# A hybrid decoder layer: the conv's taps, the sums for the FFN, the GroupNorm and one RWKV chain get other places in the order

## The chip, the cores and the metric

One core of a Trainium2 chip runs the whole kernel. The metric is the device time of one execution in microseconds (us); the time of a kernel is the median of its runs. Engines: TensorE (PE) multiplies, VectorE (DVE), ScalarE (ACT) and GpSimd (POOL) work on tiles, SyncE (SP) issues the DMA transfers. Each engine works through its own instructions in order.

## The reference, cut to what matters

One decoder layer on x of shape (1, 1024, 1024), all fp32. One combined projection feeds three groups whose outputs are concatenated and go through one output projection; a gated FFN follows.

```python
def reference(x, w_in, w_out, norm_mix, ...):
    h = rms_norm(x, norm_mix[i])
    proj = h @ w_in[i]
    p_conv, p_nsa, p_rwkv = jnp.split(proj, splits, axis=-1)
    y_conv = conv_mixer(p_conv, ...)      # GLU, depthwise conv of width 31, LayerNorm, swish
    y_nsa = nsa_mixer(p_nsa, ...)         # 8 heads, compressed + selected + sliding-window branches
    y_rwkv = rwkv7_mixer(p_rwkv, ...)     # 4 heads x 64, decay and delta rule, GroupNorm, gate
    mix = jnp.concatenate([y_conv, y_nsa, y_rwkv], axis=-1)
    x = x + mix @ w_out[i]
    h = rms_norm(x, norm_ffn[i])
    x = x + conv_ffn(h, ...)              # silu(causal_dwconv(h @ w_gate)) * (h @ w_up) @ w_down
    return rms_norm(x, norm_final)

def causal_dwconv(x, w, b):               # here k = 31, 256 channels
    y = lax.conv_general_dilated(x, w[:, None, :], window_strides=(1,), padding=[(k - 1, 0)], ...)
    return y + b
```

The RWKV step is, for each time step, S = S * w + (S @ -kk)(kk * a) + v k and y = S r; the kernel does it in chunks.

## The kernel before, in words

Every fp32 matmul of a projection is made of three passes over a high and a low part of each operand (`mm3`, L229). A weight is loaded, ACT writes its high part (`whi`, L120) and DVE the low part (`wlo`, L121); results that are kept go through the same pair on eviction (keys: L689 on ACT, L690 on DVE). A projection of 128 columns takes 24 such matmuls for each half of the 1024 time steps.

`build` walks through a list of steps: the projections (`lora`, `r0`, `keys`, `q`, `r1a`, `cmp0`, ...), and between them the RWKV steps. RWKV works on four units: head pair j (0, 1) times time half h (0, 1). For a unit `S` prepares and builds its matrices, and at its end GpSimd solves a triangular system by forward substitution, 31 rounds of a product (L532) and a sum (L534). `V` (solve) carries the result through DRAM to another layout (DVE copies `sTT`, SP stores and loads, first used at L554) and multiplies it out. `C` (chain) is the recurrence over eight chunks, each a row of PE, DVE, PE, DVE (L595, L596, L601, L608), and at its end the GroupNorm: sums and rsqrt on DVE (L621 to L632), transposes on PE (L635), gating, a store to the DRAM tensor `md` (L642).

The conv has 256 channels in two halves. Half 0 is 31 DVE taps over 1024 columns (L272). Half 1 is, for each tap, two scaled copies on ACT (`ctap`, L278, two buffers) that GpSimd adds up (L279). Then comes the LayerNorm over channels and a store to `md`. Attention goes over eight tiles of 128 queries in the order 7, 6, 5, 4, 0, 3, 2, 1; among them lie the units S10 to C11, and GpSimd makes sums of ffn_down weights (`down_sums`). The out-projection loads `mix` from `md` (L988), which holds the outputs of all three groups.

The order on each engine is set by a scheduler that puts instructions by priority and by a clock of its own; RWKV steps have a high priority, and `issue_after(ins)` keeps instructions out until `ins` has been put. So the order is fixed when the kernel is built, and an engine waits for its next instruction even if a later one could run.

## Time and profile before

| | |
|---|---|
| median of 3 runs | 1477.12 us (1475.97 to 1485.69) |
| profiled execution | 1478.54 us, span 1476.7 us |
| mean granted clock of TensorE | 0.973 |
| PE busy | 1388.3 us, 94% of the span |
| DVE / ACT / POOL busy | 1000.4 / 686.0 / 499.0 us |
| DMA | 186.69 MB, mean 126 GB/s |

The span is the profiled execution from its first instruction to its last. Times in rows are microseconds from the span's start. A busy time is the union of an engine's instructions; the granted clock is the share of full speed (2.4 GHz) that TensorE was given, so 0.50 is its lower level of 1.2 GHz. A number in brackets behind a row is the time that the engine stood idle before it, with the instruction that ended the wait.

### The profile page before, as it was taken

The page shows a single profiled execution, that of the slowest core. Times are in us where ns is not written, and L with a number is a line of the kernel's source. Part 1 is how long each engine was busy: PE and PEld are TensorE (multiplying, and loading weights), DVE is VectorE, ACT ScalarE, POOL GpSimd, SP SyncE. Part 2 cuts the span into 40 slices and gives each one's busy share as a digit, 9 for nine tenths or more (in the row PEclk, how much of TensorE's full clock was granted, in tenths as well). Part 3 has the DMA queues.
Part 4 walks back from the last instruction along what each step waited for, and adds up shares of the span by engine and source line. Part 5 has one row for each costly group of instructions (what it writes and reads, how often), then busy time and mean ns, then how long its engine had stood idle before and what let it go on. Part 6 is the DMA issues. An engine that isn't in the chain of part 4 may idle for free.

```text
span 1476.7 us, 22756 instructions
## 1 busy us (share of the span) xinstructions
PE 1388.3 (94%) x7897; PEld 1096.1 (74%) x7897; DVE 1000.4 (68%) x2187; ACT 686.0 (46%) x1377; POOL 499.0 (34%) x607
## 2 busy tenths in 40 slices
PE   6999588999799999999999899999999999999997
PEld 5887466777576676766777677888788788888886
DVE  5337594454868688798367767677775776666685
ACT  5432246634466655678333433343343334445463
POOL 1001996931153156220001144443444442113310
...
GB/s 182 44 107 83 43 103 91 148 98 168 165 33 118 98 154 119 165 158 87 229 142 64 29 94 93 113 103 69 103 112 93 108 100 166 392 277 210 190 91 114
DMA packets 206679, 186.69 MB, mean 126 GB/s; under 512 B 56355, under 2 KB 145764, under 8 KB 206564
## 3 DMA queue, kind: packets, MB, share of 16 engines
...
q14 instruction: 53, 0.43, 0.1%
...
## 4 chain that ended last, share of the span: by engine, by line
PE 78%; DVE 9%; DMA 4%; POOL 4%; ACT 3%; issue 2%; SPq 1%; DVEq 0%; ACTq 0%
PE gb L229 13%; PE mm L229 13%; PE ga L229 9%; PE rw L229 9%; PE gc L229 8%; PE tr L229 5%; PE tr L922 4%; PE av L930 4%; PE mm L897 2%; DMA mix<-md 2%; PE mm L898 2%; POOL sT L534 1%; POOL sx L532 1%; POOL cacc L279 1%; DVE pp L915 1%
## 5 line engine op out<-in xcount | busy, mean ns | idle before, releaser
L229 PE MATMUL mm<-hT,whi 128*128 128x512 f32 x608 | 200.0, 408 | 18.4 <-DVE ev L690 15.1
L229 PEld LDWEIGHTS mm<-hT,whi 128*128 128x128 f32 x608 | 115.6, 193 | 48.0 <-ACT whi L120 18.8
L229 PE MATMUL mm<-hT,wlo 128*128 128x512 f32 x304 | 123.1, 407 | 2.8 <-DVE wlo L121 2.8
L925 ACT ACTIVATE pT<-tr 128x512 f32<-128x512 f32 (+1 forms) x152 | 79.8, 536 | 58.0 <-PE tr L922 57.7
L930 PE MATMUL av<-pT,V 128*64 128x128 f32 x1056 | 97.3, 289 | 3.9 <-ACT pT L925 3.8
L922 PE MATMUL tr<-idn,pp 128*128 128x128 f32 x528 | 90.7, 290 | 1.8 <-DVE pp L915 1.8
L279 POOL TENSOR_TENSOR cacc<-cacc,ctap 128x512 f32<-128x512 f32 x60 | 85.7, 1440 | 12.6 <-ACT ctap L278 12.6
L121 DVE TENSOR_TENSOR sp<-rb,sp 128x512 fp32r<-128x512 f32 x66 | 57.0, 863 | 46.7 <-ACT sp L120 46.7
L229 PE MATMUL rw<-sp,sp 128*128 128x512 f32 x330 | 86.0, 389 | 0.0
L229 PE MATMUL tr<-sp,sp 128*128 128x512 f32 x330 | 85.9, 389 | 0.0
L930 PEld LDWEIGHTS av<-pT,V 128*64 128x64 f32 x1056 | 60.2, 138 | 30.0 <-issue 12.5
L229 PE MATMUL rw<-woh,mix 128*128 128x512 f32 x240 | 76.7, 394 | 3.7 <-DVE xn L1005 2.7
L922 PEld LDWEIGHTS tr<-idn,pp 128*128 128x128 f32 x528 | 56.2, 142 | 30.8 <-issue 29.4
L897 PE MATMUL mm<-KH,QS 128*128 128x512 f32 (+2 forms) x192 | 75.8, 401 | 3.0 <-DVE mx L901 2.5
L120 ACT ACTIVATE sp<-rb 128x512 fp32r<-128x512 f32 x66 | 41.6, 631 | 73.8 <-PE tr L229 37.5
L121 DVE TENSOR_TENSOR sp<-b,sp 128x512 fp32r<-128x512 f32 x88 | 72.1, 828 | 5.4 <-ACT sp L120 5.0
L915 DVE TENSOR_SCALAR pp<-pp,sm 128x640 f32<-128x640 f32 (+7 forms) x128 | 74.5, 622 | 1.0
L229 PEld LDWEIGHTS mm<-hT,wlo 128*128 128x128 f32 x304 | 58.7, 193 | 19.0 <-DVE wlo L121 4.6
L1084 POOL TENSOR_TENSOR S<-wraw,wr 128x512 f32<-128x512 f32 x22 | 28.5, 1297 | 127.6 <-DVE wlo L121 46.8
L229 PEld LDWEIGHTS rw<-sp,sp 128*128 128x128 f32 x330 | 62.0, 188 | 12.9
L229 PEld LDWEIGHTS tr<-sp,sp 128*128 128x128 f32 x330 | 62.0, 188 | 12.8
L532 POOL TENSOR_TENSOR sx<-sN,sT 128x60 f32<-128x60 f32 (+24 forms) x124 | 48.6, 392 | 63.6 <-DMA sN<-dn 55.5
...
## 6 DMA issues: line engine op xcount, KB each, us to landing
...
```

The source lines that it names most:

```text
L120: self.nc.scalar.activation(hi, src, AF.Copy)
L121: getattr(self.nc, eng).tensor_tensor(lo, src, hi.bitcast(F32), op=ALU.subtract)
L229: mm = lambda l, r, **k: self.nc.tensor.matmul(out, l, r, skip_group_check=more, **k)
L279: nc.gpsimd.tensor_tensor(t[:, o:o + 512], t[:, o:o + 512], z, op=ALU.add)
L532: v_.tensor_tensor(x, N[:, q, q + 1:32].unsqueeze(2).to_broadcast([P, n, w]), Tm[:, q, 0:w].unsqueeze(1).to_broadcast([P, n, w]), op=ALU.mult)
L897: pe.matmul(pts[g][:, 0:n], QS[:, r, g, :], KH[g][hf][:, ks], start=True, stop=False)
L898: pe.matmul(pts[g][:, 0:n], QS[:, r, g, :], KL[g][hf][:, ks], start=False, stop=True)
L915: v.tensor_scalar(Ps[g], Ps[g], sm[:, g:g + 1], None, op0=ALU.mult)
L922: pe.transpose(pt[:, o:o + P], Ps[g][:, kt * P:kt * P + P], self.idn)
L925: s.activation(pT[:, 0:n], pt[:, 0:n], AF.Copy)
L930: pe.matmul(av[g * 64:g * 64 + 64, r * P:r * P + P], self.V[kk // 2][:, kk % 2, vo + g * 64:vo + g * 64 + 64], pT[:, o:o + P], start=first ...
L1084: gp.tensor_tensor(t, x, y, op=op)
```

## The change

The steps are listed in another order, and four parts of the work are cut out as steps of their own:

- The 31 DVE taps are kept in a list. After each weight split two of them are put (`pace`); what is left is put at the step `cend`, where the conv's LayerNorm now is, behind `cmp0`.
- GpSimd's sums of the conv wait until the substitution of unit S00 has been put (`pa`, taps 0 to 19) or that of S01 (`pb`, taps 20 to 30). ACT's scaled copies have no such condition.
- The GroupNorm is a step `N` of its own.
- The chain C01 stands in front of `r1a` in the list, and so in front of S10.
- The sums for ffn_down wait for the substitution of S10 or S11, no longer for the softmax of the compressed branch.

```diff
-  steps="lora r0 S00 conv taps V00 S01 keys q C00 V01 r1a cmp0 r1b cmp1 r1c S10 C01 V10 S11 C10 V11 C11"
+  steps="lora r0 S00 conv taps pa V00 S01 pb keys q C00 V01 N00 C01 N01 r1a cmp0 cend r1b cmp1 r1c S10 V10 S11 C10 V11 N10 C11 N11"
...
-            self.split(hi, lo, raw)
+            ins = self.split(hi, lo, raw)
+            if self.fill:
+
+                with self.tc.issue_after(ins):
+                    for f in self.fill[:self.B["pace"]]:
+                        f()
+                    del self.fill[:self.B["pace"]]
...
+    def conv_taps(self):
+
+        nc = self.nc
+        self.cacc = [self.t4(name="cacc")[:, 0:T] for _ in range(2)]
+
+        def dve(d):
+            y, t, w = self.cy[0], self.cacc[0], self.cw[:, 0, d:d + 1]
+            if d == 0:
+                nc.vector.tensor_scalar(t, y[:, 0:T], w, self.cb[:, 0:1], op0=ALU.mult, op1=ALU.add)
+            else:
+                nc.vector.scalar_tensor_tensor(t, y[:, d:d + T], w, t, op0=ALU.mult, op1=ALU.add)
+        self.fill = [lambda d=d: dve(d) for d in range(31)]
+
+    def conv_pool(self, ds, ins):
+
+        nc = self.nc
+        y, t = self.cy[1], self.cacc[1]
+        for d in ds:
+            w = self.cw[:, 1, d:d + 1]
+            if d == 0:
+                with self.tc.issue_after(ins):
+                    nc.gpsimd.tensor_scalar(t, y[:, 0:T], w, self.cb[:, 1:2], op0=ALU.mult, op1=ALU.add)
+            else:
+                for o in (0, 512):
+                    z = self.xt([P, 512], "cv", name="ctap")
+                    nc.scalar.activation(z, y[:, o + d:o + d + 512], AF.Copy, scale=w)
+                    with self.tc.issue_after(ins):
+                        nc.gpsimd.tensor_tensor(t[:, o:o + 512], t[:, o:o + 512], z, op=ALU.add)
+
     def conv_rest(self):
         nc = self.nc
...
+        for f in self.fill:
+            f()
+        self.fill = []
+        acc = self.cacc
...
-            v_.tensor_tensor(Tm[:, q + 1:32, 0:w], Tm[:, q + 1:32, 0:w], x, op=ALU.add)
+            u.sub = v_.tensor_tensor(Tm[:, q + 1:32, 0:w], Tm[:, q + 1:32, 0:w], x, op=ALU.add).ins
...
-                with self.tc.issue_after(self.cm_ins):
+                with self.tc.issue_after(us[1, int(n > 1)].sub):
                     self.down_sums(f)
```

What the scheduler makes of it is seen in the order on the engines, at three places. Line numbers of the changed kernel are 14 to 28 higher.

ACT around the first eviction of the keys (`ev<-mm`); `whi` are weights, `ctap` scaled copies for GpSimd. Before:

```order
L120 ACTIVATE whi_2248<-wraw_2246 128x512
L278 ACTIVATE ctap_1618<-cy_1515,par 128x512
L278 ACTIVATE ctap_1621<-cy_1515,par 128x512
L278 ACTIVATE ctap_1624<-cy_1515,par 128x512
L278 ACTIVATE ctap_1627<-cy_1515,par 128x512
L689 ACTIVATE ev_2277<-mm_430_2252 128x512
L120 ACTIVATE whi_2316<-wraw_2314 128x512
```

Four scaled copies in a row stand in front of the eviction. After the change:

```order
L292 ACTIVATE ctap_1587<-cy_1515,par 128x512
L717 ACTIVATE ev_2138<-mm_402_2113 128x512
L292 ACTIVATE ctap_1590<-cy_1515,par 128x512
L120 ACTIVATE whi_2177<-wraw_2175 128x512
L292 ACTIVATE ctap_1593<-cy_1515,par 128x512
L292 ACTIVATE ctap_1596<-cy_1515,par 128x512
L120 ACTIVATE whi_2185<-wraw_2183 128x512
L717 ACTIVATE ev_2169<-mm_405_2144 128x512
L579 ACTIVATE DF<-rw_1702 32x512
```

Now one scaled copy stands in front of the first eviction, and another between that eviction and the weights of the second key projection. DF, the first result of V00, now comes two rows behind these weights' second half; before it stood among the q projections.

PE where the projections end; L617 to L637 are one chain step of C01 (before L595 to L615), L235 a projection's matmul. After the change:

```order
L235 MATMUL mm_639_3483<-hT_115,whi_3448 128x512
L235 MATMUL mm_639_3483<-hT_107,wlo_3449 128x512
L617 MATMUL rw_2824<-rH_739,AT_1868 64x128
L623 MATMUL rw_2827<-VA_1928,KB_1929 64x128 x2
L634 MATMUL rw_2823<-rH_739,rP_1867 64x128
L637 MATMUL rw_2823<-VA_1928,GR_1890 64x64
L637 MATMUL rw_2823<-VA_1928,GR_1891 64x64
L617 MATMUL rw_2835<-rH_738,AT_1868 64x128
L634 MATMUL rw_2823<-rH_738,rP_1867 64x128
L623 MATMUL rw_2838<-VA_1928,KB_1929 64x128 x2
L637 MATMUL rw_2823<-VA_1928,GR_1890 64x64
L637 MATMUL rw_2823<-VA_1928,GR_1891 64x64
```

The chain's steps follow each other with nothing between them. Before, the same steps lay in the first attention tile:

```order
L595 MATMUL rw_3625<-rH_739,AT_2077 64x128
L922 MATMUL tr_4566<-idn,pp_4541 128x128
L922 MATMUL tr_4577<-idn,pp_4541 128x128
L922 MATMUL tr_4566<-idn,pp_4541 128x128 x3
L922 MATMUL tr_4577<-idn,pp_4541 128x128 x3
L897 MATMUL mm_4775<-KH_4499,QS_4517 128x512
L898 MATMUL mm_4775<-KL_4505,QS_4517 128x512
L897 MATMUL mm_4776<-KH_4502,QS_4517 128x512
L898 MATMUL mm_4776<-KL_4508,QS_4517 128x512
L897 MATMUL mm_4783<-KH_4471,QS_4517 128x512
L898 MATMUL mm_4783<-KL_4477,QS_4517 128x512
L601 MATMUL rw_3628<-VA_2137,KB_2138 64x128 x2
```

All eight steps of C01 now follow the last projection, with ten matmuls of other work between them, and attention's first matmul (`kcmp`) stands behind the last step.

PE at the end of attention; `gyc` are the transposes of the last GroupNorm, `mix` the first matmuls of the out-projection. Before, with the last chain matmul 61 rows ahead of the transposes and the out-projection right behind these rows:

```order
L635 MATMUL rw_4413<-idn,gyc_4390 128x128 x4
L640 MATMUL rw_4421<-lora_772,lw_w 128x512
L866 MATMUL tr_7825<-idn,cmp_7702 32x128 x4
L922 MATMUL tr_7850<-idn,pp_7835 128x128 x4
L869 MATMUL av_7701<-pT_7830,vcmp_4435 128x512
L922 MATMUL tr_7878<-idn,pp_7863 128x128 x4
L930 MATMUL av_7701<-pT_7855,V_4513 64x128 x4
L922 MATMUL tr_7906<-idn,pp_7891 128x128 x4
L930 MATMUL av_7701<-pT_7883,V_4513 64x128 x4
L922 MATMUL tr_7934<-idn,pp_7919 128x128 x4
L930 MATMUL av_7701<-pT_7911,V_4513 64x128 x4
L930 MATMUL av_7701<-pT_7939,V_4513 64x128 x4
```

Ten attention rows stand behind the transposes. After the change:

```order
L897 MATMUL av_7701<-pT_7830,vcmp_4435 128x512
L950 MATMUL tr_7878<-idn,pp_7863 128x128 x4
L958 MATMUL av_7701<-pT_7855,V_4513 64x128 x4
L950 MATMUL tr_7906<-idn,pp_7891 128x128 x4
L958 MATMUL av_7701<-pT_7883,V_4513 64x128 x4
L950 MATMUL tr_7934<-idn,pp_7919 128x128 x4
L663 MATMUL rw_4413<-idn,gyc_4390 128x128 x4
L668 MATMUL rw_4421<-lora_772,lw_w 128x512
L958 MATMUL av_7701<-pT_7911,V_4513 64x128 x4
L958 MATMUL av_7701<-pT_7939,V_4513 64x128 x4
L235 MATMUL rw_8120<-woh_7950,mix_8040 128x512
L235 MATMUL rw_8120<-wol_7951,mix_8040 128x512
```

The last matmul of the chain C11 is now 11 rows ahead of the transposes, and two attention rows lie between them and the out-projection.

## Rows read from the trace of the kernel before

**Rows 1.** PE's waits, 120 to 260 us: waiter, released by, us in all, times, longest.

```profile
PE mm L229 <- DVE ev L690: 15.1, 2, 14.9
PE pm L478 <- DVE cum L476: 5.8, 1, 5.8
```

**Rows 2.** windows: length, busy (instructions) per engine, granted clock, DMA share, GB/s.

```profile
168.00:192.00 24.00, 7.80 (x19) 5.71 (x20) 10.10 (x11) 7.09 (x12) 22.51 (x37) 0.57 0.22 66
192.00:220.00 28.00, 23.80 (x119) 17.28 (x117) 27.46 (x28) 14.03 (x25) 26.29 (x21) 0.94 0.35 90
220.00:236.00 16.00, 10.17 (x53) 7.38 (x53) 10.46 (x12) 8.27 (x13) 11.64 (x9) 0.57 0.34 100
...
365.00:392.00 27.00, 17.10 (x85) 12.18 (x83) 18.70 (x63) 8.50 (x18) 5.28 (x8) 0.75 0.89 230
...
692.00:709.00 17.00, 13.01 (x115) 8.43 (x111) 8.91 (x40) 11.01 (x27) 0.81 (x2) 1.00 0.23 71
```

**Rows 3.** timeline of ACT, DVE and PE: start, us, instruction, [idle before <-releaser].

```profile
178.00 0.72 ACT L278 ACTIVATE ctap<-cy,par 128x512 f32<-128x512 f32 x1 [19.22 <-POOL cacc L279]
...
181.90 0.69 DVE L690 TENSOR_TENSOR ev<-mm,ev 128x512 fp32r<-128x512 f32 x1 [16.19 <-ACT ev L689]
...
182.73 1.19 PE L229 MATMUL mm<-hT,whi 128*128 128x512 f32 x2 [14.86 <-DVE ev L690]
```

**Rows 4.** substitution by line on POOL, 141 to 205, then 403 to 429 us.

```profile
L534 POOL TENSOR_TENSOR sT<-sT,sx 128x60 f32<-128x60 f32 (+24 forms) x31 | 22.1, 712 | 1.9
L532 POOL TENSOR_TENSOR sx<-sN,sT 128x60 f32<-128x60 f32 (+24 forms) x31 | 19.0, 614 | 44.4 <-DMA sN<-dn 42.6
...
L534 POOL TENSOR_TENSOR sT<-sT,sx 128x60 f32<-128x60 f32 (+24 forms) x31 | 10.3, 333 | 2.4
L532 POOL TENSOR_TENSOR sx<-sN,sT 128x60 f32<-128x60 f32 (+24 forms) x31 | 10.0, 323 | 13.2 <-DMA sN<-dn 10.8
```

**Rows 5.** timeline: taps and an eviction on DVE, then sums on POOL.

```profile
143.52 6.56 DVE L272 SCALAR_TENSOR_TENSOR cacc<-cy,par,cacc 128x1024 f32<-128x1024 f32 x5
...
188.19 0.68 DVE L690 TENSOR_TENSOR ev<-mm,ev 128x512 fp32r<-128x512 f32 x1
...
192.95 2.38 DVE L272 SCALAR_TENSOR_TENSOR cacc<-cy,par,cacc 128x1024 f32<-128x1024 f32 x1
...
187.61 1.80 POOL L279 TENSOR_TENSOR cacc<-cacc,ctap 128x512 f32<-128x512 f32 x1
...
190.56 1.27 POOL L279 TENSOR_TENSOR cacc<-cacc,ctap 128x512 f32<-128x512 f32 x1
...
217.59 9.36 POOL L279 TENSOR_TENSOR cacc<-cacc,ctap 128x512 f32<-128x512 f32 x6 [1.57 <-ACT ctap L278]
```

**Rows 6.** timeline: S00's result on DVE, and its first use on PE.

```profile
204.76 0.70 DVE L536 COPY sTT<-sT 128x256 f32<-128x256 f32 x1
...
214.73 0.94 PE L554 MATMUL rw<-DF,GA 32*32 32x32 f32 x24
```

**Rows 7.** PE's longest wait, 365 to 420 us.

```profile
PE rw L437 <- ACT cum L434: 3.5, 1, 3.5
```

**Rows 8.** timeline: pieces of one chain step, PE and DVE.

```profile
398.13 0.43 PE L595 MATMUL rw<-rH,AT 128*64 128x128 f32 x2
...
400.91 0.44 PE L601 MATMUL rw<-VA,KB 128*64 128x128 f32 x4
...
399.31 0.29 DVE L596 TENSOR_TENSOR VA<-rw,VA 64x128 f32<-64x128 f32 x1
...
402.66 0.57 DVE L608 SCALAR_TENSOR_TENSOR rH<-rH,rPC,rw 64x64 f32<-64x64 f32 x2
```

**Rows 9.** timeline, end of attention: DVE, then PE.

```profile
677.37 0.68 DVE L621 TENSOR_REDUCE gm<-rw 128x8 f32<-128x512 f32 x1
...
699.54 0.66 PE L635 MATMUL rw<-idn,gyc 128*128 128x128 f32 x4
...
708.93 0.50 PE L229 MATMUL rw<-woh,mix 128*128 128x512 f32 x1 [1.01 <-ACT mix L120]
```

More of the change, by code (lines that the diff above doesn't have):

```diff
@@ L23, in __init__ @@
         self.B = dict(b2=20, wraw=2, whi=2, wlo=2, t4=4, rraw=2, cy=2, hx=12, ev=3, cv=2, lora=2, rb=20, at=2, pr=7, rt=2,
-                      QS=2, pp=6, q8=2, pT=5, xn=8, ds=((), (0, 1, 2), (3, 4), (5, 6, 7), (8, 9), (10,), (), ()), h2=14, graw=2, prod=5, ft=4, u=4, wr2=4, wfh=3, wfl=3, S=2, p1=2, om=6, grow=2, pre=2, ap=(), wf=("own", "wf", "om"), hd=("vector",) * 4, tq=((0, 1, 2, 3),), ttag=("tr", "rw"),
-                      mm=3, tr=2, av=1, rw=2, mm1=2, tr1=2, pm=2, early="00 01", ga=2, gb=1, gc=1, y=16, r4=15, ta=3, tb=4, mid=2, de=dict(S3="gpsimd", T3="vector", T1="gpsimd", T2="gpsimd", T4="vector", S1="gpsimd", S2="gpsimd", S4="gpsimd"), order=(7, 6, 5, 4, 0, 3, 2, 1), sc=0, pk=1280, st="sync", last=5, sub="gpsimd",  steps="lora r0 S00 conv taps V00 S01 keys q C00 V01 r1a cmp0 r1b cmp1 r1c S10 C01 V10 S11 C10 V11 C11", both=0, cm="gpsimd", rpu=(), wo="vector", tap=(0, 31), vt="cv", vs="vector", va={1: (0, 1), 3: (2, 3), 5: (4, 5), 7: (6, 7)}, vq="sync", vl=1, vw=1, t1=("pm", "tr1"), into={6: (6, 2), 4: (4, 2), 3: (3, 1), 2: (2, 1), 1: (1, 1), 0: (0, 1)})
+                      QS=2, pp=6, q8=2, pT=5, pace=2, xn=8, ds=((), (0, 1, 2), (3, 4), (5, 6, 7), (8, 9), (10,), (), ()), h2=14, graw=2, prod=5, ft=4, u=4, wr2=4, wfh=3, wfl=3, S=2, p1=2, om=6, grow=2, pre=2, ap=(), wf=("own", "wf", "om"), hd=("vector",) * 4, tq=((0, 1, 2, 3),), ttag=("tr", "rw"),
+                      mm=3, tr=2, av=1, rw=2, mm1=2, tr1=2, pm=2, early="00 01", ga=2, gb=1, gc=1, y=16, r4=15, ta=3, tb=4, mid=2, de=dict(S3="gpsimd", T3="vector", T1="gpsimd", T2="gpsimd", T4="vector", S1="gpsimd", S2="gpsimd", S4="gpsimd"), order=(7, 6, 5, 4, 0, 3, 2, 1), sc=0, pk=1280, st="sync", last=5, sub="gpsimd",  steps="lora r0 S00 conv taps pa V00 S01 pb keys q C00 V01 N00 C01 N01 r1a cmp0 cend r1b cmp1 r1c S10 V10 S11 C10 V11 N10 C11 N11", both=0, cm="gpsimd", rpu=(), wo="vector", tap=(0, 31), vt="cv", vs="vector", va={1: (0, 1), 3: (2, 3), 5: (4, 5), 7: (6, 7)}, vq="sync", vl=1, vw=1, t1=("pm", "tr1"), into={6: (6, 2), 4: (4, 2), 3: (3, 1), 2: (2, 1), 1: (1, 1), 0: (0, 1)})
         self.B.update(bufs or {})
@@ L617, in rwkv_chain, with rwkv_norm @@
         self.H = H
+        u.py = py
+    def rwkv_norm(self, u):
+        nc = self.nc
+        v, s, pe = nc.vector, nc.scalar, nc.tensor
+        j, py = u.j, u.py
         y3 = lambda t: t.rearrange("p (a b) -> p a b", b=64)
@@ L1325, in chain, with norm @@
                 self.rwkv_chain(us[j, h])
+        def norm(j, h):
+            with self.tc.high_priority(offset=100000):
+                self.rwkv_norm(us[j, h])
         steps = dict(lora=lambda: self.rwkv_lora(hT), keys=lambda: self.attn_keys(hT), q=lambda: self.attn_q(hT),
-                     cmp=lambda: self.attn_cmp(hT), conv=lambda: self.conv_proj(hT), taps=self.conv_rest, r0=lambda: self.rwkv_proj(0, hT),
+                     cmp=lambda: self.attn_cmp(hT), conv=lambda: self.conv_proj(hT), taps=self.conv_taps, pa=lambda: self.conv_pool(range(20), us[0, 0].sub), pb=lambda: self.conv_pool(range(20, 31), us[0, 1].sub), cend=self.conv_rest, r0=lambda: self.rwkv_proj(0, hT),
                      r1=lambda: self.rwkv_proj(1, hT), cmp0=lambda: self.attn_cmp(hT, (0,)), cmp1=lambda: self.attn_cmp(hT, (1,)),
@@ L1330, in build @@
         for st in self.B["steps"].split():
-            if st[0] in "SVC" and len(st) == 3:
-                dict(S=start, V=solve, C=chain)[st[0]](int(st[1]), int(st[2]))
+            if st[0] in "SVCN" and len(st) == 3:
+                dict(S=start, V=solve, C=chain, N=norm)[st[0]](int(st[1]), int(st[2]))
             else:
```

20 lines of the change are left out of this document (2 added, 18 removed).

## The prediction

> **What bounds the kernel now.** TensorE (PE) is busy nearly all the time, so the question is where it is not. I read the waits of PE first: between 120 and 260 us its longest are 14.9 us for the keys' low half and 5.8 us for S01's preparation [rows 1]. Then the windows, which give PE's busy time and granted clock of each stretch [rows 2]. A stretch costs its length less PE's busy time (idle), and of the busy time the share by which the clock is below 1.00 (slow). 168 to 236 us: idle 16.2 + 4.2 + 5.8 = 26.2 us, slow 7.80 x 0.43 + 23.80 x 0.06 + 10.17 x 0.43 = 9.2 us, 35.4 us together. 365 to 392 us, where the projections give way to attention: idle 9.9, slow 4.3, together 14.2 us. 692 to 709 us, where attention gives way to the out-projection: idle 4.0 us at full clock. These are the places that the change touches; what it does elsewhere is hidden behind a PE that does not wait.
>
> The timeline of the long stall shows a chain of queues [rows 3]: PE has no free bank because VectorE (DVE) has not written the low half of the keys; DVE waits for ScalarE (ACT), whose eviction stands behind scaled copies `ctap`; the first of these waited 19.22 us for GpSimd to add an earlier one; and GpSimd was inside the substitution of S00. That substitution took 41.1 us of GpSimd time between 141 and 205 us (22.1 + 19.0), and the same 62 instructions of S10 took 20.3 us (10.3 + 10.0) when neither taps nor sums were beside them [rows 4].
>
> **What the change costs, part by part.** Instructions hardly change in number; order changes. The sum is made against the profiled execution, 1478.5 us, which is 1.4 us above the median of the runs before.
>
> *S00 without taps beside it, first part of the gain.* DVE's taps leave the stretch 141 to 168 us and the sums wait for the end of the substitution. It starts at 141 as before (its matrices do not move) and lasts about 20.3 us plus 5 us of hand-overs, as S10's: it ends near 166 to 168 instead of 204.7. But PE's order now puts V00's first matmuls two matmuls into the next key projection. From the copy `sTT` to the first V00 matmul it took 214.73 - 204.76 = 10.0 us through DRAM [rows 6]; nothing in the change shortens that, so PE gets there at 168.5 and waits until 176 to 178: a stall of 8.5 us (5 if SP's emptier queue helps, 15 if ACT holds the weights back as before: the third `ctap` still stands in front of `whi` and waits for GpSimd's first sum). The clock falls after such a stall: 3.4 to 4.4 us in the rows of before [rows 2], 4 taken.
>
> *Taps paced on DVE.* A tap takes 6.56 / 5 = 1.31 us alone and 2.38 us beside GpSimd's sums [rows 5]. Two behind each weight split means that about 12 fall between 168 and 212 us, all beside sums: 12 x 2.38 = 29 us, and with the evictions, splits and S01's preparation some 16 us more (24 at 0.68). That is 45 us of DVE in 44 us: DVE is as full as it was there (27.46 of 28 us, [rows 2]), and what PE waits for in it I put at 7 us (0 if the order hides it, 20 if it is as in 192 to 236 us before). Later splits have room: the taps cost nothing there because PE needs the weights one group later; without that cover each pair would cost 2.6 to 4.8 us.
>
> *The sums on GpSimd.* 38 sums at 9.36 / 6 = 1.56 us [rows 5] follow S00, then S01's substitution. Only V01 waits for these, and V01 now stands after all of q. The copy `sTT` of S01 is the danger: it waits on DVE in front of q's evictions. By the rows GpSimd is through at 168 + 61 + 25 = 254 us, near where DVE comes to it, so nothing is charged.
>
> Here a rule bears on it. The rows show that neither engine alone pays: the eviction at 188.19 took 0.68 us, as the one at 181.90 did (0.69, [rows 3]), and the sum begun at 187.61 took 1.80 us where the one at 190.56 took 1.27; at 192.95 the tap is the one that is longer [rows 5]. The Trainium skill, "SBUF — State Buffer", section "SBUF: two separate sides", says that a VectorE instruction with two SBUF inputs and a GpSimd instruction take a shared port pair as an exclusive lock, for the whole instruction, and the other fully blocks. The rows agree for a single pair. Taken at its word for the whole stretch, the work of both adds up: 38 x 1.27 + 12 x 1.31 + 24 x 0.68 = 80 us on GpSimd where the rows above give 61, S01 ends 19 us later, and DVE's copy holds q's evictions. With half of that on PE's path the sum would be 9 us longer, 1484. That is a rival below.
>
> Early gain: 35.4 - 8.5 - 4 - 7 = **16 us** (ends: 35.4 - 5 - 3 - 0 = 27; 35.4 - 15 - 4.4 - 16 = 0).
>
> *The second chain (C01) in front of attention.* Before, its steps lay between attention matmuls and cost nothing. Now the order puts all eight behind the last projection, with little of anything between. One step is 0.43 + 0.29 + 0.44 + 0.57 us [rows 8] and four hand-overs of about 0.1 (the gap between DVE's eviction and PE's restart in rows 3 is 0.14): 2.2 us, eight take 17.6 us. PE works some 9 us of it. Attention's q loads stand on SP behind the stores of the conv's second half and six loads for ffn_down, and I give them 2 us more. Idle 10.6, slow 4, and 1 for S10's preparation, whose waits (the longest 3.5 us [rows 7]) go into tile 7 where other matmuls lie between. Together 15.6 against 14.2: **-2 us** (+4 if SP and DVE are early, -14 if a step takes 4 us).
>
> *The last chain and GroupNorm (C11, N11).* Second-half steps come later in attention; at the end the last chain matmul stands 11 rows in front of the GroupNorm's transposes, where it was 61 rows. The GroupNorm's own chain is about 6 us by an estimate (five instructions on 512 columns at about 0.69 us, as rows 9 have one, and a dozen small ones; before it was begun at 677.37 and had until 699.54, [rows 9]), which those 11 rows cover. But from the transposes to the first out-projection matmul it is 708.93 - 699.54 = 9.4 us [rows 9] (eviction, gating, store to `md`, load of `mix`, split), now with two attention rows over it where there were ten. PE has 0.7 us for the transposes and, by an estimate from the same row, 0.6 for each of the three rows behind them, 2.5 us of work: idle 7.0, less the 1.0 us that it waits there now, plus a slow restart of 4.4: **-10.4 us** (-5 if the clock stays, -13 if the GroupNorm is late too).
>
> *Sums for ffn_down behind the substitutions.* In tile 0 they come nearer to the mask and softmax of the compressed branch on GpSimd: **-1 us** (0 to -4). SP: nine more entries of K and weight loads in pieces, no wait of their own.
>
> Sum: 16 - 2 - 10.4 - 1 = 2.6 us less: 1475.9 for a profiled run, **1475** on the median of the runs. The expected gain is mostly given back at the two joints of attention.
>
> **The rivals.** With 1% as what a measurement of this kernel can tell from no change, "faster" is under 1462.4 and "slower" over 1491.9.
> - *The early stalls go and the joints cost little* (0.20). For it: 35.4 us is a large pool and GpSimd was its root. Early 25, joints -1 and -6, tile 0 -1: 17 us, 1460.
> - *C01 blocks the way into attention* (0.16). Mechanism: conv LayerNorm, C01 and weight splits share DVE, and the second conv store holds the q loads on SP. A step of 4 us makes the stretch 32 us and this term -14; with a tail of -13 and an early gain of 12 it is -16: 1493. It decides if the last projection matmul and the first attention matmul are over 30 us apart. Against it: DVE was busy only 18.70 of 27 us there.
> - *The stall only moves* (0.10): ACT still holds `whi` behind `ctap`; the stall is 15 us, early gain 5: -8, 1486.
> - *The lock adds up* (0.07): 1484, as worked out.
> - Forecast (0.47): 1468 to 1482.
>
> Leaving out about 1 in 10 on either side, the range is 1459 to 1490. Faster 0.20; same 0.62 (forecast, lock, most of the moved stall); slower 0.18.
>
> **What would show it.** S00's substitution ends near 167 us and a PE wait of 8 to 9 us on the load of DF stands near 170 to 177 at the line that multiplies DF by GA; no wait of 14 us for the keys' low half. The stretch 168 to 236 us costs 15 to 22 us instead of 35. Between the last projection and the first attention matmul eight chain steps of about 2.2 us with PE half idle. In front of the out-projection a wait of about 7 us for `mix` and a clock of about 0.5 behind it. The forecast is wrong if that last wait is absent (then 1465), or if DVE's waits after 177 us are over 15 us (then 1485).

## The result, and the profile after

The changed kernel takes 1496.35 us (median of four runs, 1493.3 to 1500.6) against 1478.43 us before on the same chip: ratio 1.0116, 95% interval 1.0076 to 1.0156. It is slower by 1.2%; the forecast was 1475 us, and its range ended at 1490. The profiled execution took 1500.6 us, span 1498.8 us, so the account below is of the slowest of the four runs: 22.1 us of span where the medians differ by 17.9.

The four stretches of the program, as the windows of the profiles show them (columns as in [rows 2]), before and then after: up to the last projection matmul, to the first attention matmul, to the first matmul of the out-projection, to the end.

```profile
148.00:363.30 215.30, 188.36 (x1075) 143.80 (x1073) 125.53 (x215) 97.73 (x175) 142.32 (x185) 0.91 0.37 105
363.30:379.00 15.70, 7.84 (x66) 5.83 (x65) 6.14 (x21) 6.21 (x12) 4.50 (x11) 0.68 0.85 248
379.00:708.90 329.90, 316.56 (x2810) 229.29 (x2810) 267.57 (x930) 211.81 (x493) 111.64 (x187) 0.98 0.40 118
708.90:1476.70 767.80, 743.07 (x3268) 605.84 (x3268) 524.20 (x836) 310.35 (x563) 227.76 (x178) 0.99 0.42 138
```

```profile
148.00:359.40 211.40, 188.61 (x1101) 143.85 (x1098) 139.81 (x200) 98.19 (x174) 146.88 (x170) 0.93 0.37 101
359.40:383.80 24.40, 15.29 (x113) 11.13 (x113) 15.89 (x52) 4.17 (x9) 4.54 (x11) 0.79 0.90 259
383.80:727.20 343.40, 319.42 (x2735) 229.97 (x2735) 267.17 (x924) 215.34 (x498) 110.05 (x187) 0.97 0.38 111
727.20:1498.80 771.60, 747.00 (x3268) 608.20 (x3268) 523.77 (x836) 309.24 (x562) 228.41 (x178) 0.98 0.41 137
```

| stretch | before: us, PE idle, clock | after | difference | forecast |
|---|---|---|---|---|
| to the last projection matmul | 215.3, 26.9, 0.91 | 211.4, 22.8, 0.93 | -3.9 | -16 |
| way into attention | 15.7, 7.9, 0.68 | 24.4, 9.1, 0.79 | +8.7 | +2 |
| attention | 329.9, 13.3, 0.98 | 343.4, 24.0, 0.97 | +13.5 | +7 |
| from the out-projection on | 767.8, 24.7, 0.99 | 771.6, 24.6, 0.98 | +3.8 | +4.4 |

(The forecast's 11.4 us for the tail and the ffn_down sums are split here into 7 ahead of the out-projection, 6 of waiting for `mix` and 1 for the sums, and the slow restart, 4.4.)

The differences are of lengths; the forecast is of idle and slow time. The two differ where PE's work moves from one stretch into another, and on the way into attention they differ much: PE is busy there for 15.29 us instead of 7.84, because chain steps that lay in attention now stand in front of it.

**Where the stall was.** The timeline after, of DVE, ACT and PE around S00's end, answers to [rows 3] and [rows 6].

```profile
165.09 0.70 DVE L558 COPY sTT<-sT 128x256 f32<-128x256 f32 x1 [5.16 <-POOL sT L556]
...
170.21 0.72 ACT L292 ACTIVATE ctap<-cy,par 128x512 f32<-128x512 f32 x1 [6.53 <-POOL cacc L294]
170.84 0.61 ACT L120 ACTIVATE whi<-wraw 128x512 fp32r<-128x512 f32 x1
...
171.51 0.73 PE L235 MATMUL mm<-hT,whi 128*128 128x512 f32 x2 [4.29 <-ACT whi L120]
173.47 1.91 PE L576 MATMUL rw<-DF,GA 32*32 32x32 f32 x32 [1.23 <-DMA DF<-dt]
...
185.17 0.79 PE L235 MATMUL mm<-hT,wlo 128*128 128x512 f32 x1 [3.97 <-DVE wlo L121]
```

S00 is solved at 165 instead of 204.7. The 14.9 us of [rows 1] are gone; in their place PE waits 4.3 us for weights, behind a scaled copy on ACT that waited for GpSimd's first sum, 1.2 for DF and 4.0 for the low half of a weight. The windows that answer to [rows 2], then 236 to 280 us before and after:

```profile
168.00:192.00 24.00, 15.30 (x139) 12.04 (x140) 24.00 (x26) 12.11 (x21) 18.91 (x12) 0.72 0.41 102
192.00:220.00 28.00, 27.03 (x176) 21.07 (x174) 21.74 (x25) 17.60 (x29) 28.00 (x18) 1.00 0.28 80
220.00:236.00 16.00, 13.73 (x66) 10.22 (x66) 11.12 (x9) 9.35 (x17) 15.12 (x15) 1.00 0.44 123
...
236.00:280.00 44.00, 44.00 (x291) 34.87 (x290) 18.94 (x25) 28.85 (x49) 36.01 (x39) 1.00 0.42 129
...
236.00:280.00 44.00, 35.27 (x152) 25.96 (x153) 29.73 (x33) 13.87 (x24) 39.87 (x65) 0.86 0.39 111
```

From 168 to 236 us idle time and slow clock now cost 8.7 + 4.3, 1.0 and 2.3: 16.3 us where it was 35.4. That gain, 19 us, is real. But from 236 to 280 us, where PE was busy for all 44.00 us at full clock before, it is now idle for 8.7 and loses 4.9 to the clock: 13.6 us given back. The reason stands on GpSimd. Its groups by line from 166 to 275 us, then its first tap and a long run of sums, its substitution of S01 and DVE's taps in the timeline:

```profile
L294 POOL TENSOR_TENSOR cacc<-cacc,ctap 128x512 f32<-128x512 f32 x40 | 65.8, 1669 | 5.2 <-ACT ctap L292 5.0
L554 POOL TENSOR_TENSOR sx<-sN,sT 128x60 f32<-128x60 f32 (+24 forms) x31 | 16.3, 525 | 2.8 <-DMA sN<-dn 0.7
L556 POOL TENSOR_TENSOR sT<-sT,sx 128x60 f32<-128x60 f32 (+24 forms) x31 | 15.1, 487 | 2.1
```

```profile
165.75 2.23 POOL L288 TENSOR_SCALAR cacc<-cy,par 128x1024 f32<-128x1024 f32 x1
...
190.96 34.05 POOL L294 TENSOR_TENSOR cacc<-cacc,ctap 128x512 f32<-128x512 f32 x20 [4.71 <-ACT ctap L292]
225.74 0.46 POOL L554 TENSOR_TENSOR sx<-sN,sT 128x31 f32<-128x31 f32 x1 [0.72 <-DMA sN<-dn]
...
249.38 1.35 DVE L277 SCALAR_TENSOR_TENSOR cacc<-cy,par,cacc 128x1024 f32<-128x1024 f32 x1
...
249.72 1.16 POOL L554 TENSOR_TENSOR sx<-sN,sT 128x66 f32<-128x66 f32 x1
...
264.86 0.30 POOL L554 TENSOR_TENSOR sx<-sN,sT 128x66 f32<-128x66 f32 x1
...
272.21 0.69 DVE L558 COPY sTT<-sT 128x256 f32<-128x256 f32 x1 [9.96 <-POOL sT L556]
...
274.25 0.66 PE L617 MATMUL rw<-rH,AT 128*64 128x128 f32 x2 [6.85 <-DVE rH L630]
```

S01's substitution ran from 225.7 to 272.2 us. A product of 128x66 that takes 0.30 us alone takes 1.16 us when a tap of DVE was begun just before it: it ends at 250.9, the tap at 250.7. Eight sums stand between the first rounds; they take 11.6 of the 46.5 us, and the substitution itself 34.8 with its hand-overs. Between the end of S00 and the first product of S01 lie 30 sums, 51.2 us, and 9.5 us of other things: the first tap (2.2), waits for scaled copies (5.0), a copy, a clearing and a load. DVE comes to the copy `sTT` at 262 and waits 10 us; behind the copy stand an eviction of q and the result that PE's next chain step waits 6.9 us for. The clock is 0.50 from 275 to 280.

**The way into attention.** PE's timeline there (the last chain step but one, the last, attention's first matmul), and SP's load of q:

```profile
374.67 0.66 PE L617 MATMUL rw<-rH,AT 128*64 128x128 f32 x2
...
377.20 0.45 PE L617 MATMUL rw<-rH,AT 128*64 128x128 f32 x1 [0.36 <-DVE rH L630]
...
380.77 0.69 PE L637 MATMUL rw<-VA,GR 128*64 128x64 f32 x4
383.79 2.05 PE L871 MATMUL mm<-kcmp,q 128*128 128x128 f32 x8 [2.33 <-ACT gsq L654]
...
376.81 0.57 SPq L858 DMA_DIRECT2D q<-qd  x1
```

A chain step takes 2.5 us (377.20 - 374.67), nearly what was forecast, but the conv's and the compressed branch's transposes stand between some of them: C01 ends at 381.4, 22 us behind the last projection. Then PE waits 2.3 us for N01's square. Idle and slow time by the windows above are 7.9 + 2.5 = 10.4 us before and 9.1 + 3.2 = 12.3 after.

**The end of attention.** PE's and ACT's timeline, answering to [rows 9]; four windows around it; and PE's waits for the row maxima of the softmax, from the pages before and after:

```profile
726.48 1.39 ACT L120 ACTIVATE mix<-mix 128x512 fp32r<-128x512 f32 x2 [5.29 <-DMA mix<-md]
727.16 0.80 PE L235 MATMUL rw<-woh,mix 128*128 128x512 f32 x1 [6.67 <-ACT mix L120]
```

```profile
709.00:715.00 6.00, 5.35 (x20) 2.79 (x19) 3.62 (x16) 2.82 (x5) 0.00 (x0) 0.50 0.07 26
715.00:720.00 5.00, 5.00 (x32) 3.25 (x32) 0.69 (x1) 1.97 (x3) 0.00 (x0) 0.66 0.00 0
727.20:730.00 2.80, 2.80 (x7) 2.22 (x8) 1.33 (x2) 0.63 (x1) 0.00 (x0) 0.50 0.31 89
730.00:733.00 3.00, 3.00 (x11) 2.34 (x10) 0.74 (x2) 1.26 (x2) 0.00 (x0) 0.66 1.03 239
```

```profile
L897 PE MATMUL mm<-KH,QS 128*128 128x512 f32 (+2 forms) x192 | 75.8, 401 | 3.0 <-DVE mx L901 2.5
...
L925 PE MATMUL mm<-KH,QS 128*128 128x512 f32 (+2 forms) x192 | 76.7, 405 | 10.2 <-DVE mx L929 10.0
```

The wait for `mix` is 6.7 us where it was 1.0. Behind it the slow clock costs 1.4 + 1.0 = 2.4 us. Another 2.7 + 1.7 = 4.4 us of slow clock lie ahead of that wait: PE had stood for 2.3 of the 9 us before 709, 2.1 of them for a product of GpSimd for the compressed branch. And over the whole of attention PE waits 10.0 us for maxima, where it waited 2.5 before. These two waits, 5.7 and 7.5 us more, make up attention's 10.7 us of additional idle time; of the smaller waits some rose and some fell.

### The profile page after: what moved, and what is told of

It is laid out like the page before. It is cut to its first block, busy times and chain, and to the rows that moved or that the text cites. A ratio compares the mean times of both kernels' runs of the same rounds, so it can differ in the third digit from the quotient of the medians.

```text
span 1498.8 us, 22746 instructions
## 1 busy us (share of the span) xinstructions
PE 1401.9 (94%) x7897; PEld 1102.5 (74%) x7897; DVE 1009.8 (67%) x2187; ACT 686.6 (46%) x1377; POOL 503.1 (34%) x607
## 4 chain that ended last, share of the span: by engine, by line
PE 64%; DVE 10%; POOL 8%; DMA 4%; issue 3%; ACT 1%; SPq 1%; DVEq 0%; POOLq 0%; ACTq 0%
PE gb L235 12%; PE ga L235 9%; PE rw L235 9%; PE gc L235 8%; PE tr L235 5%; PE tr L950 4%; PE av L958 4%; PE mm L235 3%; POOL cacc L294 3%; POOL sT L556 2%; POOL sx L554 2%; PE mm L925 2%; DMA mix<-md 2%; PE mm L926 1%; DVE pp L929 1%
## 5 line engine op out<-in xcount | busy, mean ns | idle before, releaser
L235 PE MATMUL mm<-hT,whi 128*128 128x512 f32 x608 | 199.7, 410 | 7.3 <-ACT whi L120 7.2
L235 PEld LDWEIGHTS mm<-hT,whi 128*128 128x128 f32 x608 | 116.4, 195 | 36.6 <-ACT whi L120 8.5
L235 PE MATMUL mm<-hT,wlo 128*128 128x512 f32 x304 | 124.1, 411 | 5.5 <-DVE wlo L121 5.5
L294 POOL TENSOR_TENSOR cacc<-cacc,ctap 128x512 f32<-128x512 f32 x60 | 96.8, 1639 | 7.3 <-ACT ctap L292 7.0
L554 POOL TENSOR_TENSOR sx<-sN,sT 128x60 f32<-128x60 f32 (+24 forms) x124 | 45.3, 365 | 150.9 <-DMA sN<-dn 141.9
L958 PE MATMUL av<-pT,V 128*64 128x128 f32 x1056 | 93.6, 289 | 1.7 <-ACT pT L953 1.7
L235 PE MATMUL rw<-woh,mix 128*128 128x512 f32 x240 | 78.3, 402 | 9.0 <-ACT mix L120 6.7
L235 PE MATMUL rw<-sp,sp 128*128 128x512 f32 x330 | 86.2, 389 | 0.0
L235 PE MATMUL tr<-sp,sp 128*128 128x512 f32 x330 | 85.8, 389 | 0.0
L121 DVE TENSOR_TENSOR wlo<-wraw,whi 128x512 fp32r<-128x512 f32 x55 | 49.0, 891 | 45.3 <-ACT whi L120 43.1
L235 PEld LDWEIGHTS mm<-hT,wlo 128*128 128x128 f32 x304 | 59.3, 195 | 21.5 <-DVE wlo L121 7.5
L235 PEld LDWEIGHTS rw<-sp,sp 128*128 128x128 f32 x330 | 61.9, 188 | 13.1 <-DVE sp L121 0.3
L235 PEld LDWEIGHTS tr<-sp,sp 128*128 128x128 f32 x330 | 61.9, 188 | 12.9
```

Of the source, the lines that this page charges most:

```text
L121: return getattr(self.nc, eng).tensor_tensor(lo, src, hi.bitcast(F32), op=ALU.subtract).ins
L235: mm = lambda l, r, **k: self.nc.tensor.matmul(out, l, r, skip_group_check=more, **k)
L294: nc.gpsimd.tensor_tensor(t[:, o:o + 512], t[:, o:o + 512], z, op=ALU.add)
L554: v_.tensor_tensor(x, N[:, q, q + 1:32].unsqueeze(2).to_broadcast([P, n, w]), Tm[:, q, 0:w].unsqueeze(1).to_broadcast([P, n, w]), op=ALU.mult)
L958: pe.matmul(av[g * 64:g * 64 + 64, r * P:r * P + P], self.V[kk // 2][:, kk % 2, vo + g * 64:vo + g * 64 + 64], pT[:, o:o + P], start=first ...
```

## The experiments

All ratios are to the kernel before, run on the same chip, with 95% intervals. Milestones (last projection matmul, first attention matmul, first out-projection matmul) are of one profiled execution each. Executions of the kernel before, 23 in one comparison, lay between 1469 and 1485 us, so a few us of a milestone may be chance.

**Which part costs: undo one at a time.**

C01 back in attention (C01 and N01 behind S10, and N10 in front of V11):

```diff
-... V01 N00 C01 N01 r1a cmp0 cend r1b cmp1 r1c S10 V10 ...
+... V01 N00 r1a cmp0 cend r1b cmp1 r1c S10 C01 N01 V10 ...
```

> Undoes one part of the change: C01 with its GroupNorm goes back behind S10 in the list of steps, and each GroupNorm stands right behind its chain (N10 in front of V11). Taps, sums of the conv and sums for ffn_down stay as changed. Theory (four separate losses): the stretch from the last projection matmul to attention's first matmul shrinks from 24.4 us to about 16, the wait for mix in front of the out-projection from 6.7 to 0 to 2 us and the slow clock behind it goes; the wait of the chain C00 for DVE near 270 us (6.9 us) stays. Together 14 to 20 us less than the changed kernel: 1477 to 1482. Rival (the substitution of S01 holding DVE is the whole loss): at most 4 us less, 1492 to 1496.

1489.8 us, 1.0079 [1.0050, 1.0109]. Too slow for what was expected. The wait for `mix` is gone, so the places of C01 and N10 do cause it. But the way into attention is 23.4 us without C01 in it, with waits of its own:

```profile
PE mm L871 <- DMA q<-qd: 6.2, 1, 6.2
PE tr L325 <- DVE cdg L323: 4.4, 1, 4.4
PE tr L794 <- DVE hx L791: 2.8, 1, 2.8
```

The copy `sTT` on GpSimd, so that DVE needs not wait for the substitution:

```diff
-v.tensor_copy(sTT, ...)
+nc.gpsimd.tensor_copy(sTT, ...)
```

> The changed kernel with one copy on another engine: the transposed copy of the substitution's result (sTT) is made by GpSimd, right behind the substitution, and no longer by DVE. Theory: DVE's 10 us of waiting for S01's substitution goes, with PE's wait of 6.9 us for the chain C00 and the slow clock after it (4 us): 1484 to 1488. Rival (the clock and the waits between 230 and 300 us come from GpSimd's sums beside the taps, whoever copies): the wait moves to the weight splits and the time stays at 1494 to 1498.

1492.8 us, 1.0100 [1.0065, 1.0136]: the wait moves to a queue. DVE now stands 14.2 us for the stores of q, which SP holds behind S01's stores until the substitution ends:

```profile
281.02 1.67 DVE L121 TENSOR_TENSOR ev<-q,ev 128x512 fp32r<-128x512 f32 x1 [14.22 <-DMA qd<-ev]
```

The ffn_down sums at their old place:

```diff
-issue_after(us[1, int(n > 1)].sub)
+issue_after(self.cm_ins)
```

> Undoes one part of the change: the sums for ffn_down wait again for the compressed branch's softmax of their tile, not for a substitution. Theory: the late tiles lose their collisions of sums with DVE (PE's waits for the row maximum, 6.9 us between 560 and 690 us, fall to about 2.5). But the order then puts the last chain matmul directly in front of the GroupNorm's transposes, where 11 rows lay, so that PE waits there for the GroupNorm, some 6 us: 1492 to 1498. Rival (the sums cost nothing where they are): 1500 to 1504.

1516.8 us, 1.0250 [1.0209, 1.0292], 20 us worse than the change and far outside what was expected. Attention has another order once more and takes 361.7 us: PE waits 8.6 us for the last GroupNorm's `gyc`, 6.7 for `mix`, and still 8.7 for maxima. So the sums' old place does not bring the old waits back.

Fewer sums behind S00 (taps 0 to 7 instead of 0 to 19; the rest behind S01):

```diff
-range(20) ... range(20, 31)
+range(8) ... range(8, 31)
```

> The changed kernel with 8 instead of 20 GpSimd taps in front of S01's substitution (23 behind it instead of 11). Theory: 24 sums of 1.6 us leave the way of S01's substitution, which ends some 30 us earlier, so DVE's wait for it and PE's wait of 6.9 us for C00 go, with the slow clock: 10 to 12 us less; at the end of attention four rows instead of two cover the load of mix: 1 us. 1483 to 1487. Rival (the locked pair of DVE and GpSimd is what costs, wherever the sums are): 1493 to 1498.

1501.1 us, 1.0161 [1.0130, 1.0193]. S01 is solved at 251, the longest wait of C00 is 3.1 us, the projections end at 347.2: 12 us earlier than in the changed kernel and 16 earlier than before the change, as much as the prediction had put on the early part. All of it is given back: the last conv sums come later, SP stands from 361 to 379.6 us at a store of the conv in front of q, and the way into attention is 39.8 us.

The kernel before with C01 alone moved in front of `r1a`:

```diff
-... C00 V01 r1a cmp0 r1b cmp1 r1c S10 C01 V10 S11 C10 V11 C11
+... C00 V01 C01 r1a cmp0 r1b cmp1 r1c S10 V10 S11 C10 V11 C11
```

> One part of the change alone: the kernel before, with C01 (and its GroupNorm) in front of the projections of the second unit instead of behind S10. Theory (C01's place brings all steps of the second half later, so that the last GroupNorm and the out-projection's load of mix are no longer covered): the order puts the last chain matmul directly in front of the GroupNorm's transposes and two rows in front of the out-projection. PE waits there some 6 us for the GroupNorm and 6.5 for mix, at half clock behind: 12 to 17 us more than before, 1489 to 1495. Rival (the end of attention is not what costs, the early part is): 1475 to 1480.

1488.3 us, 1.0047 [1.0021, 1.0073]. PE's waits at the end of attention in this kernel:

```profile
PE rw L635 <- DVE gyc L632: 8.5, 1, 8.5
PE rw L229 <- ACT mix L120: 6.3, 1, 6.3
```

This shows the tail by itself: the place of C01 makes the last chain late at the out-projection; taps, sums and GroupNorm steps are not needed for it. The loss, about 7 us, is half of the 12 to 17 expected: attention with both waits in it is 337.6 us long against 329.9, as the work of C01 now lies ahead of it.

**The conv's stores on SP.** In the next runs the stores of the conv's output go over ACT's queue:

```diff
-self.st.dma_start(self.md[:, j, sl], th)
+nc.scalar.dma_start(self.md[:, j, sl], th)
```

With C01 back as well:

> C01 and the GroupNorms back as in e1_c01_back, and the four stores of the conv's output to md issued by ACT instead of SP. Theory: the way into attention is held by SP, whose q loads stand behind the last two of these stores (issued at 369 and 373 us). Without them SP issues the q loads by about 368: PE's wait of 6.2 us for q goes, and the stretch from the last projection to attention falls from 23.4 to about 17 us; what stays is PE's wait of 4.4 + 2.8 us for the conv's LayerNorm and the second compressed branch. 1489.8 falls to about 1483. Rival (DVE's and ACT's work on the LayerNorm is what holds attention, the stores only follow it): the stretch stays at 22 to 24 us, 1488 to 1491.

In the changed kernel alone:

> The changed kernel with the conv's four stores to md issued by ACT instead of SP, C01 where the change has it. Theory: SP passes q's loads some 3 us earlier, but the eight steps of C01 still lie in front of attention and the end of attention keeps its wait for mix (two rows of cover, 6 to 7 us): 0 to 6 us less than the changed kernel, 1490 to 1496. Rival (the stores alone made the difference between e1_c01_back and e5_c01_stores_act): 12 us less, 1484.

With C01 back and 8 taps behind S00, and with C01 back and 13:

> C01 and GroupNorms back, stores on ACT, 8 instead of 20 GpSimd taps in front of S01's substitution. Theory: the early part ends near 347 us as in e4_fewer_sums_first, 6 us earlier than in e5_c01_stores_act; the conv's LayerNorm comes later (last sum near 326 us), but nothing on SP stands behind it. 1466 to 1474. Rival (the later sums hold PE's LayerNorm matmuls, which stand in the projections and in front of attention): 1478 to 1488.

> As e11_c01_stores_act_fewer_sums with 13 taps in front of S01's substitution: its end moves from 272 to about 260 us, in front of the point where DVE's copy and SP's stores come to it, and the last sum to about 315 us. Theory: PE's wait for C00 (6.5 us) goes and the LayerNorm is not late: 1468 to 1473. Rival as there: 1476 to 1484.

With C01 back they take the loss away: 1478.0 us, 0.9996 [0.9967, 1.0025]; with 13 taps 1478.6 us, 0.9989 [0.9967, 1.0011]; with 8 taps 1494.0, 1.0094 [1.0058, 1.0130]. Alone they do nothing: 1497.3, 1.0108 [1.0065, 1.0150], with 7.4 us of wait for `mix`. So the loss goes only with both, C01's place and the stores; but two versions that end the projections 10 us earlier than the kernel before are not faster than it. Nor did the stores act as expected: against the version with C01 back alone, the way into attention became longer (30.0 us against 23.4), and the gain stands in the projections (354 against 359) and in attention (318.7 against 338.7). Why is not shown. The windows of the version with 20 taps, on the way into attention and in attention:

```profile
353.80:383.80 30.00, 17.10 (x75) 11.58 (x73) 21.05 (x68) 8.59 (x18) 4.41 (x11) 0.72 0.93 263
383.80:702.50 318.70, 312.12 (x2793) 227.73 (x2792) 258.15 (x912) 212.64 (x489) 109.70 (x188) 0.99 0.38 115
```

The way in is 30.0 us, not the 17 expected: S10's preparation stands in front of attention, and PE waits 9.5 us for its `cum`.

With 13 taps S01 is solved at 255.3, 17 us earlier than in the changed kernel, and yet the projections end within 1 us of the version with 20. The cost has only moved: PE still waits 4.4 us behind the copy `sTT`, and from 255 to 280 us DVE is then busy for 24.1 of 25 us, its taps beside GpSimd's sums, with 3.1 us more of waiting for a chain step in that queue.

**The conv's LayerNorm earlier** (`cend` in front of `cmp0`, C01 back), then with 8 taps behind S00, then with `sTT` on GpSimd:

> C01 and the GroupNorms back, and the conv's LayerNorm one projection earlier (in front of cmp0 instead of behind it). Theory: with the conv's last sum at 307 us the LayerNorm and its stores are over before the last projection ends; the stretch to attention falls to 16 us, as in the kernel before. The order also brings the last chain matmul 80 rows ahead of the GroupNorm's transposes and leaves 25 rows in front of the out-projection, so no wait for mix. 1476 to 1482: the early loss (C00 waiting for S01's substitution) stays. Rival (the LayerNorm waits for GpSimd's sums wherever it stands, and holds PE in the projections instead): 1486 to 1492.

> As e6_c01_conv_earlier, with 8 instead of 20 GpSimd taps in front of S01's substitution. Theory: DVE's wait for S01's substitution goes, the last projection ends near 347 to 350 us as in e4_fewer_sums_first; but GpSimd's last sum comes near 326 us and the LayerNorm waits for it, so the stretch to attention is 18 to 25 us. 1466 to 1476. Rival (what is saved early is given back in front of attention, as in e4_fewer_sums_first): 1478 to 1486.

> As e6_c01_conv_earlier, with the transposed copy of the substitution's result made by GpSimd. Theory: the early part ends near 354 us as in e2_stt_pool, the stretch to attention is about 16 us, the end of attention as before: 1470 to 1476, the first version not slower than the kernel before. Rival: 1480 to 1486, if what is saved early comes back in front of attention.

1502.7 (1.0161 [1.0124, 1.0197]), 1508.0 (1.0197 [1.0163, 1.0231]) and 1485.6 us (1.0038 [1.0006, 1.0069]). With `cend` there, the taps that are left and the LayerNorm stand ahead of the compressed branch, and the projections end at 380, 387 and 373 us instead of 359. Only the third comes near the kernel before.

**What holds the way into attention.** In the changed kernel, in seven of the versions above and in the kernel before, the first attention matmul stands at 377 to 384 us, whether the projections end at 353 or at 363; in the other five it stands at 387 to 410. Two causes were left: SP's queue and the DMA engines (share 0.90 to 0.93 there), or chains on DVE and ACT. First, sixteen of the 32 K loads go over GpSimd's queue:

```diff
-nc.sync.dma_start(t[d * 64:...], self.kd[b, z, ...])
+(nc.sync, nc.gpsimd)[z].dma_start(t[d * 64:...], self.kd[b, z, ...])
```

> The changed kernel; the sixteen loads of the keys' low parts (KL) go through GpSimd's queue instead of SP's. Theory 'SP's queue holds the way into attention': the sixteen entries took about 0.62 us each on SP, so the q loads, at 376.8 in the changed kernel, come about 10 us earlier, and the first attention matmul (383.8) follows as far as the chain C01, whose last matmul stands in front of it at 380.8, lets it: C01's own steps lie behind conv stores and w2, so 2 to 6 us earlier, 1490 to 1495 us. Rival 'DVE and ACT hold it' (conv LayerNorm, the compressed keys, C01's steps): q moves, but the first attention matmul stays within 2 us of 383.8 and the time at 1496 (within 0.2%).

> The version with C01 back, the conv's stores on ACT's queue and 13 sums behind S00, with the KL loads on GpSimd's queue. There the first attention matmul waited 4.7 us for q (loaded at 370.9) and stood at 378.3, although the projections ended at 352.8. Theory 'SP's queue': the wait for q goes, the first attention matmul comes at 372 to 374, and the time is 1471 to 1475 us. Rival 'DVE and ACT hold it': another wait (the compressed branch's hx, at 370.7 there) takes its place, first attention matmul at 377 or later, time unchanged at 1478.

> The version with C01 back and the conv's stores on ACT's queue, with the KL loads on GpSimd's queue. There S10's preparation stood in front of attention and PE waited 9.5 us for DVE's cum, which waits for loads of r and k that stand among the K loads on SP. Theory 'SP's queue': these loads come earlier, the stretch from the last projection matmul to the first attention matmul falls from 30.0 to about 22 us, and the time to 1470 to 1473 us. Rival 'DVE and ACT hold it': the stretch stays at 28 to 31 us and the time at 1478.

> The kernel before, with the KL loads on GpSimd's queue alone. Its stretch is 15.7 us with waits of 3.5 and 3.0 us for S10's cum and 0.6 for q. Theory 'SP's queue': q and the loads of r and k come earlier, 3 to 5 us of the stretch's 7.9 us of idle time go: 1473 to 1476 us. Rival 'DVE and ACT hold it': within 0.15% of the kernel before.

1501.8 (1.0156 [1.0131, 1.0181]), 1479.6 (1.0026 [1.0001, 1.0051]), 1476.7 (1.0003 [0.9979, 1.0027]) and 1495.2 us (1.0107 [1.0075, 1.0138]); first attention matmul at 383.6, 388.6, 384.3 and 380.9, where the same versions without this edit had 383.8, 378.3, 383.8 and 379.0. No start came earlier by more than 0.2 us, one came 10 us later: SP's queue in entries is not the bound. In the kernel before, SP's loads now wait for earlier transfers, and its load of q is issued at 373.4, where it was at 374.5:

```profile
SPq L708 <- DMA KH<-kd: 3.8, 4, 1.6
```

The Trainium skill, "Trainium Kernel Development and Optimization", section "Key Constraints", says that queues of several engines share the same 16 DMA engines and that a second one saves only issue time; these runs agree: in the kernel before, q was issued 1.1 us earlier and PE could start with it 1.9 us later, at 380.9, after a wait of 7.3 us.

Then half the bytes: each K tile is loaded once and copied by GpSimd, idle there, to the other 64 partitions.

```diff
+if d == 0:
+    nc.sync.dma_start(t[0:64], self.kd[b, z, ...])
+else:
+    nc.gpsimd.tensor_copy(t[64:128], t[0:64])
```

> The kernel before; each K tile is loaded from DRAM once, and GpSimd, idle there, copies it into the other 64 partitions, so sixteen of the 32 K loads and half of their bytes go (2.1 MB, some 9 us at the 233 GB/s of 350 to 380 us). Theory 'the DMA engines are full on the way into attention' (their share was 0.77, 0.76 and 0.90 from 350 to 380 us): the waits for S10's cum (3.5 and 3.0, behind its loads of r and k) and for q get shorter, first attention matmul at 372 to 376 instead of 379.0, time 1472 to 1475. Rival 'the chains on DVE and ACT hold it': first attention matmul at 378 or later, time within 0.15% of the kernel before.

> The version with C01 back, the conv's stores on ACT's queue and 13 sums behind S00, each K tile loaded once and copied by GpSimd. There PE waited 4.1 us for hx and 4.7 us for q (loaded at 370.9), first attention matmul at 378.3. Theory 'the DMA engines are full': the wait for q goes and the first attention matmul comes at 371 to 374, time 1472 to 1475. Rival 'the chains on DVE and ACT hold it': first attention matmul at 377 or later, time 1477 to 1480.

1490.3 (1.0072 [1.0044, 1.0101]) and 1488.0 us (1.0053 [1.0026, 1.0079]), both slower than either expectation. In the kernel before q is now issued 9.4 us earlier, and S10's waits stay as they were (3.4 and 3.0 us, before 3.5 and 3.0), as its timelines of SP and PE show:

```profile
365.02 0.57 SPq L833 DMA_DIRECT2D q<-qd  x1
...
371.04 1.87 PE L437 MATMUL rw<-bones,cum 128*128 128x2 f32 x8 [3.42 <-ACT cum L434]
375.91 1.11 PE L446 MATMUL rw<-idn,cum 128*128 128x128 f32 x4 [3.00 <-DVE cum L443]
```

Attention starts at 376.8, 15.3 us behind the last projection matmul (15.7 before). In the other version it starts at 376.4, 1.9 us earlier than without the copy, with waits of 5.0 us for `hx` and 4.6 for `cum`. So entries hold nothing of the way in, and bytes 2 us at most. What is left are the chains on DVE and ACT that stand in front of attention in PE's order, and PE's waits name them: S10's preparation, the compressed keys, the conv's LayerNorm, or C01. No run made these chains shorter, so this is by elimination. The time was lost behind them: attention took 341.8 and 341.9 us, where the same versions without the copy had 329.9 and 328.6.

**Attention's own order.** The kernel before with K loads on GpSimd shows something else. Its edit touches no attention instruction, and the projections and the way in take 214.7 and 18.2 us (215.3 and 15.7 before); but attention takes 346.9 us instead of 329.9:

```profile
380.90:727.80 346.90, 326.20 (x2814) 236.84 (x2814) 275.12 (x931) 213.59 (x495) 110.46 (x187) 0.95 0.37 109
```

The scheduler has made another order: of PE's rows from the first attention matmul to the out-projection, about two thirds can be found in the same sequence as before. The same edit left the order on PE nearly as it was (98 rows of 100) in the version with C01 back and the stores on ACT's queue, and there attention took 321.1 us against 318.7. With 13 taps the order changed again, and attention became shorter, 319.1 against 328.6. So some 10 to 17 us of attention can come or go with an order that no one chose; an effect on attention of this size or less cannot be told from the order by these runs.

## Why the prediction was wrong, point by point

**The step that failed first: "GpSimd is through at 168 + 61 + 25 = 254 us ... so nothing is charged."** It was through at 272, while DVE came to the copy `sTT` at 262. The 61 us for the sums were near (38 at 1.56 are 59): they took 62.8. The 25 us were not: they are S10's price, with nothing beside it, and the same change lets DVE's taps run beside S01, which took 34.8 us. And 9.5 us had no term: the first tap on GpSimd, its waits for scaled copies, and smaller things. S00 ended 3 us early, which took some of it back. A row for a substitution with taps beside it was at hand, 41.1 us for S00 [rows 4]. It would have given 168 + 61 + 41 = 270, but that close only by luck: 6 us too much for S01 against the missing 9.5. The early gain was 3.9 us instead of 16, which is 12 of the 24.7 us between forecast and profile; the version with 8 taps, where S01 ends at 251, ends the projections 16 us earlier than before the change. The other early terms held in sum: S00 solved at 165 (forecast 166 to 168), stall and slow clock from 168 to 236 us 16.3 us (forecast 19.5). But the stall of 8.5 us that was put on DF was 1.2 there; the other 8.3 came for halves of weights.

**The rule that was given 7%.** The Trainium skill, "SBUF — State Buffer", section "SBUF: two separate sides", is the rule by which DVE's two-input instructions and GpSimd's block each other whole. In the small the rows agree, 0.30 against 1.16 us. The rival built on it gave S01 19 us later than 254, and it was 18, but the agreement of these two numbers is luck: the rival put the 19 us into the sums, 80 us for 61, and they took 62.8; the delay came from S01's own small instructions and from the 9.5 us that neither forecast had. Its place on PE's path was right, and the early loss against the forecast (12 us) near the 9 that it gave. With 13 taps ahead of it S01 ended 17 us earlier, and other chain steps waited in DVE's queue instead.

**C01 in front of attention: about right in the forecast's own measure.** Idle and slow time there rose by 1.9 us (forecast 2). The stretch grew by 8.7 because PE's work moved into it, and it stayed under the 30 us that the rival had named. A step was priced well (2.5 us against 2.2); what stands between the steps, and N01's square behind them, was not. What was not foreseen is that attention gained nothing by the work that left it: PE was busy in it for 319.4 us instead of 316.6. Attention's order changed as well, so why it did not gain stays open. And C01 is not the only thing that can fill the stretch: with C01 back in attention it is 23.4 us.

**The tail: the wait right, the clock in part.** 6.7 us of wait against 7.0, and shown alone by moving C01 in the kernel before. Behind it the stretch to the end is 3.8 us longer against 4.4, but only 2.4 of that is the slow restart.

**Sums for ffn_down: -1 us forecast.** PE's waits for maxima rose by 7.5 us. It is not the sums' place that sets them: with the sums back at their old place they are 8.7 us, in the kernel before with K loads on GpSimd 13.4, and with the sums as changed, C01 back and the stores on ACT's queue 2.8. They come and go with attention's order. The rows are from the pages of these three, in this sequence:

```profile
L925 PE MATMUL mm<-KH,QS 128*128 128x512 f32 (+2 forms) x192 | 78.7, 415 | 9.5 <-DVE mx L929 8.7
...
L897 PE MATMUL mm<-KH,QS 128*128 128x512 f32 (+2 forms) x192 | 79.0, 416 | 13.5 <-DVE mx L901 13.4
...
L925 PE MATMUL mm<-KH,QS 128*128 128x512 f32 (+2 forms) x192 | 75.5, 399 | 2.8 <-DVE mx L929 2.8
```

So the part of the +13.5 in attention that is not the wait for `mix` has no cause shown here.

Of the signs named in advance, the wait for `mix` was there. PE's waits for DVE between 177 us and the end of the projections were 14.4 us, just short of the 15 that were to mean 1485, and 6.9 of them are the one wait behind S01's copy. The wait of 8 to 9 us for DF, named as a sign of being right, did not come.
